# The last of seven down products moved behind the classical rest, and the memory sums in half-size transfers over more of the layer

## The chip, the cores and the metric

The kernel runs on one core of one Trainium2 chip. The metric is device time in microseconds of one execution; lower is better. Besides the times there is one profiled execution with its trace, on which the figures below rest.

## The reference

A two-layer encoder over 512 rows of width 1024, in float32. Each layer, cut to what matters here:

```
h   = rms_norm(x, pre_mix_norm)
q, k, v, u, B, C = split(h @ w_in)            # 6 x 512 columns
attn = dilated_mixture_attention(rotary(q), rotary(k), v)
conv = B * short_conv(C * u)
x   = x + rms_norm(concat(rms_norm(attn), rms_norm(conv)) @ w_out, post_mix_norm)
g, u = split(rms_norm(x, pre_ffn_norm) @ w_gate_up)      # 2 x 2816 columns
x   = x + rms_norm((silu(g) * u) @ w_down, post_ffn_norm)
```

## The kernel before

**Numbers and tiles.** Rows are held in four tiles of 128 (t = 0 to 3), the width in eight k tiles, the hidden width of 2816 in 22 tiles m. Every factor is split in two fp32r parts, hi and lo, so a product of two tiles is three matmuls (hi by hi, hi by lo, lo by hi). Weights arrive as halves of 128 x 1024 float32, 512 KB: `load_raw` issues the load on the SP queue (line 122), `split_half` makes hi on ScalarE (line 221) and lo on VectorE (line 222). Three raw buffers and four buffers each of hi and lo rotate. `take_half` splits up to two halves ahead of the one it returns, and `split_half` loads up to two halves ahead of that; the argument `keep` names the oldest half that must stay because a later row tile reads it again.

**Who orders what.** TensorE and SP run in the order in which the code issues their work. The order on ScalarE, VectorE and POOL is set by a planner that simulates costs, with program order as priority; instructions under `keep_in_program_order` stay in order among themselves.

**The layer's stages.** The input projection begins with the values (function `values`, called for a row tile and a half of the k tiles), goes on with four pairs of query/key tiles and six pairs of convolution tiles, and runs attention in steps in between: each k step calls `advance`. Then come the output projection, the gate/up product and the down product. The gate/up product takes tiles m = 0 to 3 classically and m = 4 to 21 by seven products of half size in place of eight (function `seven`, matmuls at line 900); for each such m two halves are loaded and seven weight operands are made.

**The down product.** The first 16 of the 22 hidden tiles also go by seven products of half size (function `partial`, matmuls at line 994), the other six (the rest, `REST = 6`) classically (line 1056), into the same PSUM banks. A block (two row tiles by 512 columns) of the output is called c11, c12 (rows 0 and 1, first and second half of the columns), c21, c22 (rows 2 and 3). Product p = 0 to 6 holds 48 matmuls over eight k tiles for two row tiles. The activation operands of product p are made by `operands(p)` while product p-1 runs; product six adds to c21 only. `rest_splits` splits the activations of the six rest tiles. After product six the rest runs for f = 0, 1 (column halves) and t = 0 to 3, 18 matmuls each; after each the block is evacuated (square with row sum, multiplication with the gain); after f = 1 the row tile is finished: scale, residual (line 689), and where a layer follows, its norm (`normed`, lines 292 and 294).

**The turn to the next layer.** `transposed` turns one row tile of the normalised rows with eight transposes on TensorE (line 301), and splits the result (lines 305, 306). Row tiles 0 and 1 are turned in the rest pass f = 1, after three hidden tiles of t = 2 and of t = 3. Row tiles 2 and 3 are turned in the next layer's values, in the calls (0, 1) and (1, 1) after two k tiles.

**The memory sums.** Four of the seven weight operands of the down product are sums of weight blocks. They are made in device memory: t1 = b11 + b12, t3 = b12 + b22, t2 = t1 + b22, t4 = t2 + b21, by transfers from memory to memory that POOL issues, some plain, some adding (`weight_sums`). A block is 2 MB and goes in two transfers of 1 MB, 16 transfers a layer. So that they don't start at once, each is tied to a place in SP's order: SP issues a load of four bytes (`due`, line 158, into a slot of the pool `small`, which the softmax and the norms use too), POOL copies it (line 159) and then issues the transfer (line 160). `feed_forward` calls `next(adding)` after each of the 18 seven-product tiles.

Of the kernel before, what the change touches and what calls it, by code (L numbers as in the profile page):

```python
# [36 lines left out]
KS = 8  # L37
SB = 7 * KS // 2
REST = MT - 2 * KS
EPS = 1e-6  # L40
MAGIC = 12582912.0

# [40 lines left out]
def encoder(ctx: ExitStack, tc: tile.TileContext, x, xT, pos, mask, cols, rows, w, wd, out):  # L83
# [48 lines left out]
    def weight_source(i):  # L132

        l, r = divmod(i, 2 * NCHUNK)
        if r < 2 * NW:
            return w[l * NW + r // 2][:, (r % 2) * 1024:(r % 2) * 1024 + 1024]
        p, q = divmod(r - 2 * NW, KS // 2)
        if p < 7:
            src = (lambda: down_quarter(l, 0, 0), lambda: tsum[l][:, 0, :], lambda: tsum[l][:, 1, :],
                   lambda: down_quarter(l, 1, 0), lambda: tsum[l][:, 2, :], lambda: down_quarter(l, 1, 1),  # L140
                   lambda: tsum[l][:, 3, :])[p]()
            return src[:, q * 1024:q * 1024 + 1024]
        c = 4 * KS * 512 + (r - 2 * NW - SB) * 1024
        return wd[l][:, c:c + 1024]

    def weight_sums(l):

        b11, b12, b21, b22 = (down_quarter(l, g, f) for g in range(2) for f in range(2))  # L150
        t1, t2, t3, t4 = (tsum[l][:, k, :] for k in range(4))
        for pairs in (((t1, b11), (t3, b12)), ((t1, b12), (t3, b22)), ((t2, t1),), ((t2, b22),), ((t4, t2),), ((t4, b21),)):
            for n, (o, src) in enumerate(pairs):
                for c in range(0, KS * 512, 2048):
                    add = {"accum_op": ALU.add} if src is b22 or src is b21 or (src is b12 and o is t1) else {}
                    due = small(1)[:1]
                    seen = sb.tile([1, 1], F32, tag="seen", bufs=2, name=nm("seen"))
                    nc.sync.dma_start(due, cols[0:1, 0, 0:1])
                    tc.keep_in_program_order(nc.gpsimd.tensor_copy(seen, due))
                    tc.keep_in_program_order(nc.gpsimd.dma_start(o[:, c:c + 2048], src[:, c:c + 2048], **add))  # L160
                    yield

    tc.keep_in_program_order(nc.scalar.preload_act_table_set("trig_and_small"))
# [120 lines left out]
    def new_hT():  # L284
        return [[big([P, 4, S], F32R) for _ in range(2)] for _ in range(2)]
# [11 lines left out]
    def transposed(t, h, hT, tag, raw=None):  # L297
        for g in range(2):
            b = bank(tag)
            for k in range(4):  # L300
                nc.tensor.transpose(b[:, k * P:(k + 1) * P], h[:, (4 * g + k) * P:(4 * g + k + 1) * P], ident)
            b4 = b.rearrange("p (k t) -> p k t", k=4)
            hi = hT[0][g][:, :, t * P:(t + 1) * P]
            lo = hT[1][g][:, :, t * P:(t + 1) * P]
            nc.scalar.copy(hi, b4)
            nc.vector.tensor_sub(lo, b4, hi.bitcast(F32))
            if raw is not None:
                nc.scalar.copy(raw[g][:, :, t * P:(t + 1) * P], b4)
# [288 lines left out]
                nc.scalar.activation(V[:, t, :], accs[t], AF.Copy, scale=inv[:, 2 * t:2 * t + 1])  # L597
        return inv

    def in_proj_attention(l, hT, h, tables):  # L600

        base = l * NCHUNK
        V = big([P, NT, S])
# [2 lines left out]
        def values(t, g, turn=None):  # L606
            if accs[t] is None:
                accs[t] = bank("acc")
            for kt in range(4 * g, 4 * g + 4):
                if turn is not None and kt == 4 + TURN // 2:  # L610
                    transposed(turn, h[turn], hT, "acc")
                hi, lo = take(base + g, (kt % 4) // 2, 2 * base if t < NT - 1 else None)
                c = (kt % 2) * 512
                mm3(accs[t], hT[0][g][:, kt % 4, t * P:(t + 1) * P], hT[1][g][:, kt % 4, t * P:(t + 1) * P],
                    hi[:, c:c + 512], lo[:, c:c + 512], kt == 0, kt == KT - 1)
            if g == 1:
                nc.scalar.copy(V[:, t, :], accs[t])

        inv = None
        if l == 0:  # L620
            inv = first_values(hT, V)
            nc.sync.dma_start(mask_sb, mask)
        else:
            for o in [(0, 0), (0, 1, 2), (1, 0), (1, 1, 3), (2, 0), (2, 1), (3, 0), (3, 1)]:
                values(*o)

        qks = [None] * 4
# [4 lines left out]
        count = [0]  # L632

        def advance():
            for _ in range(PACE[count[0] % len(PACE)]):
                next(att, None)
            run_background(BG)
            count[0] += 1
# [104 lines left out]
    def feed_forward(l, hT, hs, raw, adding):  # L743
# [35 lines left out]
        def gated_full(m, accs):  # L779
            sg = tmp([P, S])  # L780
            nc.scalar.activation(sg, accs[0], AF.Silu)
            gated(m, sg, accs[1])
# [159 lines left out]
        for m in range(3):  # L942
            pair_part(base + m, accs[m], hT, HS, S, step, keep if m == 0 else None)
            gated_full(m, accs[m])
        ahead = None
        for m in range(3, SEVEN):
            n = [0]
# [38 lines left out]
        def partial(p, outs, start, ahead):  # L986
            hi_t, lo_t = seconds.pop(p)
            for k in range(KS):
                wh, wl = take_half(d0 + p * (KS // 2) + k // 2)
                c = (k % 2) * 512  # L990
                for i in range(2):
                    st = slice(i * P, i * P + P)
                    for n, (sh, mh) in enumerate(((hi_t, wh), (hi_t, wl), (lo_t, wh))):
                        nc.tensor.matmul(outs[i], sh[:, k, st], mh[:, c:c + 512], start=start and k == 0 and n == 0,  # L994
                                         stop=False, skip_group_check=True)
                next(ahead, None)
            for _ in ahead:
                pass

        def rest_splits():  # L1000
            for m in range(2 * KS, MT):
                split(m)
                yield
# [23 lines left out]
        c22.extend((written("att", 5), written("pv", 5)))  # L1027
        for i in range(2):
            nc.vector.tensor_sub(c22[i], p5[i], c21[i])
        partial(5, c12, False, operands(6))  # L1030
        for i in range(2):
            nc.vector.tensor_sub(c12[i], c12[i], u2[i])
        partial(6, c21, False, rest_splits())
        accs = [c11 + c21, c12 + c22]

        def evac(f, t, acc):
            j = row([P, S])
            nc.scalar.activation(j, acc, AF.Square, accum_out=ssq[t][:, f:f + 1])
            fx[f][t] = (row if f else tmp)([P, S])
            nc.vector.tensor_mul(fx[f][t], acc, gpost[:, f * 512:f * 512 + 512])  # L1040

        log_table()
        for f in range(2):
            if f == 1 and gnext is not None:
                hT = new_hT()
            for t in range(NT):
                for m in range(2 * KS, MT):
                    j = f * REST + m - 2 * KS
                    if m == 2 * KS + TURN_D and f == 1 and gnext is not None and t >= 2:
                        transposed(t - 2, hs[t - 2], hT, "acc")  # L1050
                        hs[t - 2] = None
                    wh, wl = take_half(d0 + SB + j // 2, d0 + SB + f * REST // 2 if t < NT - 1 else None)
                    c = (j % 2) * 512
                    hi, lo = act_dst(m)
                    for n, (sh, mh) in enumerate(((hi, wh), (hi, wl), (lo, wh))):
                        nc.tensor.matmul(accs[f][t], sh[:, t * P:(t + 1) * P], mh[:, c:c + 512], start=False,  # L1056
                                         stop=m == MT - 1 and n == 2, skip_group_check=True)
                evac(f, t, accs[f][t])
                if f == 0:
                    part0[t] = mean_part(ssq[t][:, 0:1], D)  # L1060
                else:
                    r = rsqrt_mean(ssq[t][:, 1:2], D, part=part0[t])
                    residual(t, fx, r)
                    if gnext is not None:
                        hs[t] = normed(t, gnext)
                    else:
                        nc.sync.dma_start(out[t * P:(t + 1) * P, :512], x_sb[t][:, :512])
                        nc.scalar.dma_start(out[t * P:(t + 1) * P, 512:], x_sb[t][:, 512:])
        return hT, hs

    with tc.manual_schedule(engines={mybir.EngineType.PE, mybir.EngineType.SP}):
        warm_up()
        hs = [None] * NT
        hT = new_hT()
        tables = None
        for l in range(DEPTH):
            adding = weight_sums(l)
            merged, sq_a, sq_c, tables, inv = in_proj_attention(l, hT, hs, tables)
            hT, hs, raw = out_proj(l, merged, sq_a, sq_c, inv)
            hT, hs = feed_forward(l, hT, hs, raw, adding)  # L1080

# [87 lines left out]
```

## Time and profile before

| what | value |
|---|---|
| time, median of three runs | 1168.9 us (1167.38 to 1169.53) |
| the profiled execution: time / span | 1170.38 us / 1168.4 us |
| granted TensorE clock, mean | 0.997 |
| busy: TensorE / VectorE / ScalarE / POOL | 98% / 72% / 57% / 6% of the span |
| moved by DMA | 162.64 MB, mean 139 GB/s |
| memory sums in it: plain or adding from the weights / from a sum | 24 / 8 transfers of 1 MB, two layers |

The span is from the first to the last instruction. In a row of the TensorE timeline stand the start, the duration, the line, the operation with output and inputs, and in brackets the idle time before it with what ended it; matmuls are pipelined, so a row's duration is longer than the distance to the next start. A row of a window shows its length, then the busy time and count of TensorE, its weight loads, VectorE, ScalarE and POOL, then the granted clock, the share of the DMA engines and GB/s. A row of waits has the total, the number and the longest. A row of the chain of waits has the start, the length and what the chain ran through.

### The profile page before, as it was taken

Reading aid. Unit: us, or ns where it says so; the run is one execution under the profiler, and the core shown is the slowest. Engines: PE = TensorE matmul, PEld = TensorE weight load, DVE = VectorE, ACT = ScalarE, POOL = GpSimd, SP = SyncE. Lnnn points to the kernel's source line nnn. Section 1 sums busy time; section 2 is a strip of 40 time slices with the busy share of each in tenths; the row PEclk is TensorE's granted clock in tenths of the full one; section 3 lists DMA queues with packets and bytes.
Section 4 is the critical chain, followed back from the end, with each engine's and each line's share of the span. In section 5 each row is a group of like instructions: output and inputs, shape, how many; then the busy total and the mean of one; then the engine's idle time right before and its main releaser. Section 6 shows DMA issues by size and latency. Waiting matters only on the chain.

```text
span 1168.4 us, 18250 instructions
## 1 busy us (share of the span) xinstructions
PE 1148.5 (98%) x7008; PEld 1010.5 (86%) x7008; DVE 841.4 (72%) x1392; ACT 669.8 (57%) x1263; POOL 70.0 (6%) x127
## 2 busy tenths in 40 slices
PE   9999999999999999999999999999999999999997
PEld 8777778899999999888777777788999999998886
DVE  5798664776886778984757986448767777789844
ACT  7577544564655656663545775446545556567632
POOL 6000011000010000000000000110000011000000
PEclk9999999999999999999999999999999999999999
DMA  8221234222677777665223212441136776676641
GB/s 323 91 72 55 73 90 126 74 73 90 206 185 191 213 216 181 217 203 176 69 66 100 73 55 72 126 125 53 59 125 193 203 196 182 207 181 213 198 144 73
DMA packets 41911, 162.64 MB, mean 139 GB/s; under 512 B 4960, under 2 KB 4960, under 8 KB 37728
## 3 DMA queue, kind: packets, MB, share of 16 engines
q1 hardware_dynamic: 35344, 122.64, 32.8%
q0 software_dynamic: 5760, 37.75, 13.7%
q8 instruction: 55, 0.90, 0.3%
q10 hardware_dynamic: 720, 1.09, 0.3%
q14 instruction: 32, 0.26, 0.1%
HBM read 159.36 MB, written 35.65 MB: 167 GB/s over the span
## 4 chain that ended last, share of the span: by engine, by line
PE 44%; DVE 3%; DMA 2%; ACT 1%; issue 1%; DVEq 0%; ACTq 0%; SPq 0%
PE acc L900 7%; PE att L900 6%; PE acc L250 5%; PE acc L251 5%; PE acc L252 5%; PE acc L994 5%; PE att L994 2%; DMA raw<-in_w 2%; PE acc L1056 1%; PE pv L487 1%; PE att L480 1%; PE att L1056 1%; PE att L250 1%; PE att L252 1%; PE att L251 1%
## 5 line engine op out<-in xcount | busy, mean ns | idle before, releaser
L222 DVE TENSOR_TENSOR wl<-raw,wh 128x1024 fp32r<-128x1024 f32 x140 | 170.7, 1220 | 79.3 <-ACT wh L221 78.2
L900 PE MATMUL acc<-big,wh 128*128 128x256 f32 x1152 | 212.2, 283 | 0.0
L221 ACT CAST wh<-raw 128x1024 fp32r<-128x1024 f32 x140 | 146.9, 1051 | 108.8 <-PE acc L251 35.9
L900 PEld LDWEIGHTS acc<-big,wh 128*128 128x128 f32 x1152 | 179.8, 192 | 0.2
L900 PE MATMUL acc<-big,wl 128*128 128x256 f32 x576 | 163.7, 284 | 2.8 <-DVE wl L821 2.8
L900 PE MATMUL att<-big,wh 128*128 128x256 f32 x864 | 160.7, 283 | 0.2 <-ACT att L908 0.2
L250 PE MATMUL acc<-big,wh 128*128 128x512 f32 (+1 forms) x400 | 154.0, 385 | 0.0
L252 PE MATMUL acc<-big,wl 128*128 128x512 f32 (+1 forms) x400 | 149.5, 374 | 0.0
L251 PE MATMUL acc<-big,wh 128*128 128x512 f32 (+1 forms) x400 | 149.3, 373 | 0.0
L900 PEld LDWEIGHTS att<-big,wh 128*128 128x128 f32 x864 | 134.6, 192 | 0.5 <-ACT att L908 0.4
L900 PE MATMUL att<-big,wl 128*128 128x256 f32 x432 | 123.2, 285 | 0.4
L820 ACT CAST wh<-t 128x512 fp32r<-128x512 f32 x144 | 88.7, 619 | 45.8 <-PE att L900 30.7
L900 PEld LDWEIGHTS acc<-big,wl 128*128 128x128 f32 x576 | 110.5, 192 | 3.9 <-DVE wl L821 3.7
L821 DVE TENSOR_TENSOR wl<-t,wh 128x1024 fp32r<-128x1024 f32 x72 | 87.7, 1218 | 17.3 <-ACT wh L820 17.3
L994 PE MATMUL acc<-wh,big 128*128 128x512 f32 x320 | 99.5, 389 | 0.0
L820 ACT CAST wh<-raw 128x512 fp32r<-128x512 f32 x108 | 63.4, 619 | 47.0 <-PE acc L900 31.3
L252 PEld LDWEIGHTS acc<-big,wl 128*128 128x128 f32 x400 | 75.3, 188 | 13.9
L250 PEld LDWEIGHTS acc<-big,wh 128*128 128x128 f32 x400 | 75.4, 189 | 12.3 <-issue 0.8
L251 PEld LDWEIGHTS acc<-big,wh 128*128 128x128 f32 x400 | 75.6, 189 | 11.6
L900 PEld LDWEIGHTS att<-big,wl 128*128 128x128 f32 x432 | 82.8, 192 | 2.2 <-DVE wl L821 2.2
L821 DVE TENSOR_TENSOR wl<-raw,wh 128x512 fp32r<-128x512 f32 x72 | 68.5, 951 | 6.2 <-ACT wh L820 6.0
L994 PEld LDWEIGHTS acc<-wh,big 128*128 128x128 f32 x320 | 60.1, 188 | 12.4
(265 smaller groups left out, 2225.5 us busy)
## 6 DMA issues: line engine op xcount, KB each, us to landing
raw<-in_w SPq DMA_DIRECT2D x144, 512.0 KB
tsum<-in_wd POOLq DMA_DIRECT2D x24, 1024.0 KB, 8.1
raw<-in_wd SPq DMA_DIRECT2D x36, 512.0 KB
raw<-tsum SPq DMA_DIRECT2D x32, 512.0 KB
tsum<-tsum POOLq DMA_DIRECT2D x8, 1024.0 KB, 5.3
gain<-in_rows SPq DMA_DIRECT2D x7, 512.0 KB
big<-in_xT SPq DMA_DIRECT2D x8, 256.0 KB
raw<-in_w SPq DMA_DIRECT2D x8, 256.0 KB
```

Source lines behind the costliest of these rows:

```text
L221: nc.scalar.copy(hi, raws[i])
L222: nc.vector.tensor_sub(lo, raws[i], hi.bitcast(F32))
L250: nc.tensor.matmul(o, sh, mh, start=start, stop=False)
L251: nc.tensor.matmul(o, sh, ml, start=False, stop=False)
L252: nc.tensor.matmul(o, sl, mh, start=False, stop=stop)
L480: nc.tensor.transpose(tp[:, k * P:(k + 1) * P], sm[:, k * P:(k + 1) * P], ident)
L487: nc.tensor.matmul(o[hd * 64:hd * 64 + 64, half * 256:half * 256 + 256], V[:, k, hc:hc + 64], PT[hd][:, k, :], start=k == 0, stop=k == NT - 1)
L820: nc.scalar.copy(hi[:, c:c + 512], src[:, c:c + 512])
L821: nc.vector.tensor_sub(lo[:, :n], src[:, :n], hi[:, :n].bitcast(F32))
L900: nc.tensor.matmul(o[:, :HS], sh[:, c], mh[:, k, :], start=start and k == 0 and n == 0, stop=k == 3 and n == 2, skip_group_check=True)
L994: nc.tensor.matmul(outs[i], sh[:, k, st], mh[:, c:c + 512], start=start and k == 0 and n == 0, stop=False, skip_group_check=True)
L1056: nc.tensor.matmul(accs[f][t], sh[:, t * P:(t + 1) * P], mh[:, c:c + 512], start=False, stop=m == MT - 1 and n == 2, skip_group_check=True)
```

## The change

The change has two parts.

First, the down product: the rest now runs right after product five, f = 0 and then f = 1, and product six comes last, its two row tiles (t = 2 and t = 3, columns of f = 0) one after the other, 24 matmuls each with the four weight halves held for both. Row tiles 0 and 1 are finished in the rest pass f = 1 as before; row tiles 2 and 3 are evacuated for f = 1 there and finished after their part of product six. Row tiles 0 and 1 are turned in the middle of product six's first and second part, row tiles 2 and 3 in the values of the next layer at (1, 0) and (2, 0), after two k tiles; the banks for the turned rows come from the tag `att` and no more from `acc`. The order in which the weight halves are loaded follows (`SR`), and `before_rest` makes the operands of product six and the rest splits during product five.

Second, the memory sums: 32 transfers of 512 KB a layer in place of 16 of 1 MB, in the same order, and 11 of them are tied to steps of the input projection (every sixth `advance`), 3 to the tiles m = 0 to 2 of gate/up, 18 to the seven-product tiles.

```diff
     def weight_source(i):
...
-        p, q = divmod(r - 2 * NW, KS // 2)
+        r -= 2 * NW
+        if SR <= r < SR + REST:
+            c = 4 * KS * 512 + (r - SR) * 1024
+            return wd[l][:, c:c + 1024]
+        p, q = divmod(r if r < SR else r - REST, KS // 2)
...
     def weight_sums(l):
-                for c in range(0, KS * 512, 2048):
+                for c in range(0, KS * 512, 1024):
...
-                    tc.keep_in_program_order(nc.gpsimd.dma_start(o[:, c:c + 2048], src[:, c:c + 2048], **add))
+                    tc.keep_in_program_order(nc.gpsimd.dma_start(o[:, c:c + 1024], src[:, c:c + 1024], **add))
                     yield
...
         def values(t, g, turn=None):
-                if turn is not None and kt == 4 + TURN // 2:
-                    transposed(turn, h[turn], hT, "acc")
+                if turn is not None and kt == TURN // 2:
+                    transposed(turn, h[turn], hT, "att")
...
-            for o in [(0, 0), (0, 1, 2), (1, 0), (1, 1, 3), (2, 0), (2, 1), (3, 0), (3, 1)]:
+            for o in [(0, 0), (0, 1), (1, 0, 2), (1, 1), (2, 0, 3), (2, 1), (3, 0), (3, 1)]:
                 values(*o)
...
         def advance():
+            if count[0] % 6 == 5:
+                next(adding, None)
...
         for m in range(3):
             pair_part(base + m, accs[m], hT, HS, S, step, keep if m == 0 else None)
             gated_full(m, accs[m])
+            next(adding, None)
...
-        partial(5, c12, False, operands(6))
+        def before_rest():
+            for _ in operands(6):
+                yield
+            for _ in rest_splits():
+                yield
+
+        partial(5, c12, False, before_rest())
         for i in range(2):
             nc.vector.tensor_sub(c12[i], c12[i], u2[i])
-        partial(6, c21, False, rest_splits())
         accs = [c11 + c21, c12 + c22]
...
+        def finished(t, f):
+            r = rsqrt_mean(ssq[t][:, f:f + 1], D, part=part0[t])
+            residual(t, fx, r)
+            if gnext is not None:
+                hs[t] = normed(t, gnext)
+            else:
+                nc.sync.dma_start(out[t * P:(t + 1) * P, :512], x_sb[t][:, :512])
+                nc.scalar.dma_start(out[t * P:(t + 1) * P, 512:], x_sb[t][:, 512:])
+
+        def turned(t):
+            if gnext is not None:
+                transposed(t, hs[t], hT, "att")
+                hs[t] = None
...
         for f in range(2):
             for t in range(NT):
                 for m in range(2 * KS, MT):
-                    if m == 2 * KS + TURN_D and f == 1 and gnext is not None and t >= 2:
-                        transposed(t - 2, hs[t - 2], hT, "acc")
-                        hs[t - 2] = None
-                    wh, wl = take_half(d0 + SB + j // 2, d0 + SB + f * REST // 2 if t < NT - 1 else None)
+                    wh, wl = take_half(d0 + SR + j // 2, d0 + SR + f * REST // 2 if t < NT - 1 else None)
...
-                evac(f, t, accs[f][t])
-                if f == 0:
+                if f == 0 and t < 2:
+                    evac(0, t, accs[0][t], tmp)
                     part0[t] = mean_part(ssq[t][:, 0:1], D)
+                elif f == 1:
+                    evac(1, t, accs[1][t], row if t < 2 else tmp)
+                    if t < 2:
+                        finished(t, 1)
+                    else:
+                        part0[t] = mean_part(ssq[t][:, 1:2], D)
+
+        if gnext is not None:
+            hT = new_hT()
+        hi_t, lo_t = seconds.pop(6)
+        for i in range(2):
+            for k in range(KS):
+                if k == KS // 2:
+                    turned(i)
+                wh, wl = take_half(d0 + SR + REST + k // 2, None if i else d0 + SR + REST)
+                c = (k % 2) * 512
+                st = slice(i * P, i * P + P)
+                for n, (sh, mh) in enumerate(((hi_t, wh), (hi_t, wl), (lo_t, wh))):
+                    nc.tensor.matmul(c21[i], sh[:, k, st], mh[:, c:c + 512], start=False,
+                                     stop=k == KS - 1 and n == 2, skip_group_check=True)
+            evac(0, 2 + i, c21[i], row)
+            finished(2 + i, 0)
         return hT, hs
```

More of the change, by code (lines that the diff above doesn't have):

```diff
@@ L39 @@
 REST = MT - 2 * KS
+SR = 6 * KS // 2
 EPS = 1e-6
@@ L142, in weight_source @@
             return src[:, q * 1024:q * 1024 + 1024]
-        c = 4 * KS * 512 + (r - 2 * NW - SB) * 1024
-        return wd[l][:, c:c + 1024]
     def weight_sums(l):
@@ L598, in first_values, with in_proj_attention @@
         return inv
-    def in_proj_attention(l, hT, h, tables):
+    def in_proj_attention(l, hT, h, tables, adding):
         base = l * NCHUNK
@@ L1029, in feed_forward, with evac @@
             nc.vector.tensor_sub(c22[i], p5[i], c21[i])
-        partial(5, c12, False, operands(6))
+        def before_rest():
[4 more added lines that the diff above has]
+        partial(5, c12, False, before_rest())
         for i in range(2):
             nc.vector.tensor_sub(c12[i], c12[i], u2[i])
-        partial(6, c21, False, rest_splits())
         accs = [c11 + c21, c12 + c22]
-        def evac(f, t, acc):
+        def evac(f, t, acc, tag):
             j = row([P, S])
             nc.scalar.activation(j, acc, AF.Square, accum_out=ssq[t][:, f:f + 1])
-            fx[f][t] = (row if f else tmp)([P, S])
+            fx[f][t] = tag([P, S])
             nc.vector.tensor_mul(fx[f][t], acc, gpost[:, f * 512:f * 512 + 512])
+        def finished(t, f):
[10 more added lines that the diff above has]
+                hs[t] = None
         log_table()
         for f in range(2):
-            if f == 1 and gnext is not None:
-                hT = new_hT()
             for t in range(NT):
@@ L1056, in feed_forward @@
                         nc.tensor.matmul(accs[f][t], sh[:, t * P:(t + 1) * P], mh[:, c:c + 512], start=False,
-                                         stop=m == MT - 1 and n == 2, skip_group_check=True)
-                evac(f, t, accs[f][t])
-                if f == 0:
+                                         stop=(f == 1 or t < 2) and m == MT - 1 and n == 2, skip_group_check=True)
+                if f == 0 and t < 2:
+                    evac(0, t, accs[0][t], tmp)
                     part0[t] = mean_part(ssq[t][:, 0:1], D)
[L1061 to L1065, printed above, removed]
-                    else:
-                        nc.sync.dma_start(out[t * P:(t + 1) * P, :512], x_sb[t][:, :512])
-                        nc.scalar.dma_start(out[t * P:(t + 1) * P, 512:], x_sb[t][:, 512:])
+                elif f == 1:
+                    evac(1, t, accs[1][t], row if t < 2 else tmp)
+                    if t < 2:
+                        finished(t, 1)
+                    else:
+                        part0[t] = mean_part(ssq[t][:, 1:2], D)
[14 more added lines that the diff above has]
+            finished(2 + i, 0)
         return hT, hs
@@ L1077, in encoder @@
             adding = weight_sums(l)
-            merged, sq_a, sq_c, tables, inv = in_proj_attention(l, hT, hs, tables)
+            merged, sq_a, sq_c, tables, inv = in_proj_attention(l, hT, hs, tables, adding)
             hT, hs, raw = out_proj(l, merged, sq_a, sq_c, inv)
```

## The prediction

> **What bounds the kernel now.** I read the head of the page first, then the list of what TensorE waited for over the whole run.
>
> ```profile
> span 1168.4 us, 18250 instructions
> ...
> PE 1148.5 (98%) x7008; PEld 1010.5 (86%) x7008; DVE 841.4 (72%) x1392; ACT 669.8 (57%) x1263; POOL 70.0 (6%) x127
> ```
>
> ```profile
> PE acc L301 <- DVE small L273: 3.6, 2, 2.1
> PE acc L900 <- DVE wl L821: 2.8, 4, 1.0
> PE acc L301 <- DVE small L269: 1.5, 3, 1.2
> ```
>
> TensorE sets the time, and no change that leaves its matmuls alone can win more than its holes. The three longest entries stand in two places: L301, the transposes that carry the normalised rows into the next layer, and L900, the seven-product part of gate/up. A busy figure hides slow matmuls, so I measured both places by their start times, with the TensorE timeline, the chain of waits and the windows by stage.
>
> **Place one, the border between the layers**, from the first rest matmul of layer 0 (L1056) to the first matmul after the values of layer 1:
>
> ```profile
> 545.78 0.39 PE L1056 MATMUL acc<-wh,big 128*128 128x512 f32 x1
> ...
> 573.98 1.06 PE L301 MATMUL acc<-ident,mid 128*128 128x128 f32 x8 [1.51 <-DVE small L273]
> ...
> 580.36 1.07 PE L301 MATMUL acc<-ident,mid 128*128 128x128 f32 x8 [1.21 <-DVE small L269]
> ...
> 589.78 1.49 PE L301 MATMUL acc<-ident,mid 128*128 128x128 f32 x8 [2.13 <-DVE small L273]
> ...
> 597.80 1.03 PE L301 MATMUL acc<-ident,mid 128*128 128x128 f32 x8
> 598.60 0.47 PE L250 MATMUL acc<-wh,big 128*128 128x512 f32 x1
> ...
> 610.96 0.39 PE L250 MATMUL acc<-big,wh 128*128 128x512 f32 x1
> ```
>
> ```profile
> 590.00:594.00 4.00, 4.00 (x16) 3.36 (x15) 3.04 (x7) 2.44 (x7) 0.00 (x0) 0.57 0.27 103
> ```
>
> ```profile
> 1128.87 16.32 PE acc L1056 x72
> ...
> 1161.55 0.69 ACT row L1038 x2
> ```
>
> The undisturbed pace is 16.32 / 72 = 0.2267 us a matmul. The stretch holds 144 rest and 96 value matmuls, 54.4 us, and four turns of eight transposes, which cost 0.88 us each where nothing waits (598.60 - 597.80, and 0.08 for the slower matmul behind): 57.9 us. It took 610.96 - 545.78 = 65.2 us. The loss is **7.25 us**: 4.85 us of waiting before three turns, and most of the rest is the clock, granted at 0.57 from 590 to 594 us, right behind the 2.13 us hole.
>
> **Place two, the 18 seven-product tiles of each layer**, first and last matmul of both layers, the pace in a clean part, one window of it, and the queues:
>
> ```profile
> 284.98 0.40 PE L900 MATMUL acc<-big,wh 128*128 128x256 f32 x2
> ```
>
> ```profile
> 468.69 0.40 PE L994 MATMUL acc<-wh,big 128*128 128x512 f32 x1
> ```
>
> ```profile
> 864.85 0.40 PE L900 MATMUL acc<-big,wh 128*128 128x256 f32 x2
> ```
>
> ```profile
> 1051.61 0.40 PE L994 MATMUL acc<-wh,big 128*128 128x512 f32 x1
> ```
>
> ```profile
> 875.09 2.88 PE acc L900 x24
> ...
> 885.17 2.88 PE acc L900 x24
> ...
> 1025.62 7.25 DMA raw<-in_w
> ```
>
> ```profile
> 870.00:960.00 90.00, 90.00 (x752) 90.00 (x751) 67.65 (x94) 53.21 (x116) 8.40 (x18) 1.00 0.69 194
> ```
>
> ```profile
> 357.99 3.31 SPq L122 DMA_DIRECT2D raw<-in_w  x2
> 361.35 0.28 SPq L158 DMA_DIRECT2D small<-in_cols  x1
> 369.38 3.31 SPq L122 DMA_DIRECT2D raw<-in_w  x2
> ```
>
> ```profile
> tsum<-in_wd POOLq DMA_DIRECT2D x24, 1024.0 KB, 8.1
> ```
>
> A clean tile takes 885.17 - 875.09 = 10.08 us, so 18 take 181.4 us. Layer 0 took 183.7 and layer 1 186.8: losses of **2.27 and 5.32 us**. Their cause is the supply of weights. The SP queue issued its weight pairs 11.39 us apart (357.99 to 369.38) where a tile lasts 10.08. Such a pair waits for a buffer, lands beside a 1 MB memory sum (8.1 us to land) and is split; prefetch covers this for a while, and then the chain shows a load of 7.25 us on the path. The two places hold 14.84 us together.
>
> **The change part by part.** *Matmuls.* None is added or removed: 48 matmuls of product six run after the rest passes as two groups of 24, one per row tile. The pace of a product is that of the rest, 10.88 us for 48 in the row below and 0.2267 us each, so 0.
>
> *The rest begins one product earlier.* Its operands must be split during product five instead of six, on top of the operands of product six. These rows say whether that time is there, the last rest split on VectorE and product five's start in layer 1:
>
> ```profile
> 1095.54 1.28 DVE L757 TENSOR_TENSOR big<-mid,big 128x512 fp32r<-128x512 f32 x2
> ```
>
> ```profile
> 1107.11 10.88 PE att L994 x48
> ```
>
> The planner already put the last rest split at 1096.8, 10 us before product five even begins and 21 us before the rest would begin now (1107.11 + 10.88). Cost 0; without that lead it would be at most the six splits, 6 x 0.64 = 3.9 us a layer.
>
> *Where the rows are turned.* What counts is the distance, in TensorE work, from a tile's last matmul to its transposes. Before, t=0 had 18 + 9 matmuls (6.1 us), t=1 the same and a turn (7.0), t=2 36 and a turn (9.0), t=3 42 and a turn (10.4). After, t=0 is finished in the second rest pass and turned in the middle of product six's first half: 54 + 12 matmuls, 15.0 us; t=1 has 36 + 24 + 12 and a turn, 17.2 us; t=2 and t=3, finished by product six, have 54 and a turn each, 13.1 us. The work between, from the square on ScalarE to the normalised rows on VectorE, is shown by the first and the last tile:
>
> ```profile
> 566.44 0.60 ACT L1038 ACTIVATE row<-att 128x512 f32<-128x512 f32 x1 [2.43 <-PE att L1056]
> ```
>
> ```profile
> 572.55 1.28 DVE L294 SCALAR_TENSOR_TENSOR mid<-x,small,gain 128x1024 f32<-128x1024 f32 x1
> ```
>
> ```profile
> 583.54 0.60 ACT L1038 ACTIVATE row<-pv 128x512 f32<-128x512 f32 x1 [0.32 <-PE pv L1056]
> ```
>
> ```profile
> 595.35 1.28 DVE L294 SCALAR_TENSOR_TENSOR mid<-x,small,gain 128x1024 f32<-128x1024 f32 x1
> ```
>
> It took 7.4 us for t=0 (566.44 to 573.83) and 13.1 us for t=3 (583.54 to 596.63), with VectorE crowded. Before, every distance lay under its need or near it; after, t=0 and t=1 have twice the need and t=2, t=3 just the crowded one. All four holes should close, and the slow clock with them.
>
> What is late next is VectorE. Before, the last rest tile ran on weights split long before; now four halves of product six and four of the values follow each other at 1.36 us of TensorE each (product six holds each half for 6 matmuls at a time), so about seven splits of 1.2 us fall into the 20 us in which three rows are normalised. It was tight already: in the before run a split ended at 586.18 and the matmul that reads it started at 586.29.
>
> ```profile
> 584.95 1.23 DVE L222 TENSOR_TENSOR wl<-raw,wh 128x1024 fp32r<-128x1024 f32 x1
> ```
>
> ```profile
> 586.29 0.44 PE L251 MATMUL acc<-wl,big 128*128 128x512 f32 x1
> ```
>
> I bound what stays of place one between 0 (all hidden) and 5 us (each of seven splits one 0.69 us VectorE operation late) and take **1.5**, nearer to nothing, since the distances of the rows leave the planner room to put splits first.
>
> *The memory sums.* Before, 16 transfers of 1 MB a layer fell into 18 tiles; after, 11 of 32 halves go out in the input projection, 3 before the tiles and 18 in them: 9 MB of 16. In the clean window 194 GB/s moved; the weights are 1 MB a tile, 104 GB/s, the sums the other 90. At 9/16 they move 51, together 155. A load that lands in 7.25 us beside them scales to 5.8 us; the worst loop of 11.39 us becomes about 9.9, under the 10.08 of TensorE. That is the good end. Against it, other POOL transfers of 512 KB landed hardly faster than 1 MB:
>
> ```profile
> wk<-in_w POOLq DMA_DIRECT2D x4, 512.0 KB, 6.1
> big<-in_w POOLq DMA_DIRECT2D x4, 512.0 KB, 5.0
> ```
>
> But landing time holds latency in which nothing moves, and what delays a weight is the moving. I keep **2.0 us** of the 7.59, between 0 (every loop under 10.08) and 7.6 (nothing changes), nearer to the bytes because the stage is full of them.
>
> The Trainium skill speaks against this edit: "DMA: Bandwidth & Descriptors", sections "Anatomy of one DMA" and "Rules for kernel authors", gives a POOL transfer a fixed 2 us beside its bytes and asks for 1 MiB or more. By its formula 512 KB is 3.2 us and 1 MB 4.4, so the sums in a tile would fall only from 16/18 x 4.4 = 3.9 to 3.2 us and most of place two would stay. The two rows above lean its way.
>
> *What the input projection gets.* Eleven sums a layer move to a stage whose engines look like this in layer 1, and so do eleven small loads on SP, each followed by a copy and an issue on POOL:
>
> ```profile
> 620.00:740.00 120.00, 119.34 (x629) 93.96 (x628) 95.56 (x213) 81.68 (x154) 5.53 (x5) 1.00 0.21 66
> ```
>
> DMA is at 0.21 and POOL at 5.5 of 120 us, so the transfers are covered; uncovered, one would delay a weight half by at most its own 8.1 us. Queued behind a POOL wait are the additions of squares, first needed by the row scales after the stage. I take 0.5 us for both layers, between 0 and 2. In layer 1 the SP queue also stands at the output stores of t=0 and t=1 before it issues product six's last half; that half is first read 36 + 18 matmuls, 12.2 us, after t=1's last one, and the whole longer chain to normalised rows took 7.4, so 0.
>
> *The tail.* From the last matmul (square at 1161.55) to the end are 6.85 us of the same operations as before: 0.
>
> **Sum:** 14.84 - 1.5 - 2.0 - 0.5 = 10.8 us less. The profiled execution was 1170.38 us, 2.0 beyond its span; it would become 1159.6. The median of the runs shown, 1168.9, is 1.5 us below that execution and becomes **1158.1**.
>
> **The rivals.**
>
> *VectorE takes over at the border.* The end of place one's estimate: 5 us stay, gain 10.8 - 3.5 = 7.3, **1161.6 us**. For it: the split that was 0.1 us early. Against: t=0 and t=1 no longer compete there.
>
> *Half the size, not half the time.* If a 512 KB sum holds the DMA engines as long as a 1 MB one, place two stays whole: 10.8 - 5.6 = 5.2, **1163.7 us**. For it: each tile still carries one sum, and the 5.0 and 6.1 us above. Against: the stage moved bytes at 194 GB/s, so bytes count there. This is the course that the Trainium skill's "DMA: Bandwidth & Descriptors" points to.
>
> *SP held in the input projection, slower.* Each sum's small load takes a slot of the pool that the softmax uses, and SP issues in order: a load that stands for such a slot holds the weights behind it. The SP queue's waits and the end of the stage:
>
> ```profile
> SPq L122 <- DVE small L473: 72.6, 8, 11.7
> ```
>
> ```profile
> 774.41 0.79 PE att L544 x8
> ```
>
> SP already stands up to 11.7 us at a softmax operation. From 610.96 to 774.41 are one pair of halves without attention (10.9 us), nine with it and 24 matmuls (5.4 us): 16.3 us a pair, 8.2 a half. A hold longer than that is paid by TensorE, 11.7 - 8.2 = 3.5 us each time. Four hits of 22 more than eat the gain; seven, 24.5 us, make **1182.6 us**. For it: the pool is shared. Against: 24 slots reach eight scores back, and TensorE lost under 1 us of 120 in the window above.
>
> **How the numbers follow.** Forecast 0.70, VectorE 0.12, size 0.11, SP held 0.05, and 0.02 that small gains and small holds cancel. The low end is every hole closed: 1168.9 - 14.8 = 1154.1. Both milder rivals together would leave 10.8 - 3.5 - 5.6 = 1.7, 1167.2 us; I stop the range at 1166, a little inside. 1154 to 1166 then holds the forecast and each milder rival alone. 0.2%, 2.3 us, is about what a measurement of this kernel can tell from no change: faster 0.91, within it 0.03, slower 0.06.
>
> **What would show it.** In the changed profile the waits at L301's transposes should be gone or under 0.5 us each, and no border window should show a clock under 1.00. From the first rest matmul to the first after the values there are then 288 matmuls and four turns, 65.3 + 3.5 = 68.8 us; up to 71 is as forecast. Each seven-product stage should last under 183 us, with SP's pairs about 10.1 us apart, and the input projection should keep its length to 1 us. Wrong would be waits on weight splits at product six or the values (the first rival), stages of 184 and 187 us with loads on the chain (the second), or an input projection longer by several us behind SP (the third).

## The result, and the profile after

The changed kernel takes **1157.8 us** (median of 4 runs, 1157.5 to 1157.9) against 1168.7 us before (4 runs on the same chip): a ratio of 0.9907, 95% interval 0.989 to 0.9924. The forecast was 1158.1 us, between 1154 and 1166.

What TensorE waited for, in the changed kernel; L305 is now the line of the transposes and L906 that of the seven-product tiles:

```profile
PE acc L255 <- DVE wl L226: 1.3, 1, 1.3
...
PE acc L305 <- DVE small L273: 0.4, 2, 0.2
```

The three longest entries of before are gone: L906 is not in the list at all, and the 0.4 us before transposes lie in the output projections, none at this border. One new entry has come, 1.3 us for a weight split.

The border between the layers, from the first rest matmul to the first matmul after the values, on the TensorE timeline (start, duration, line, operation):

```profile
532.33 0.39 PE L1001 MATMUL att<-wh,big 128*128 128x512 f32 x1
532.56 0.39 PE L1079 MATMUL acc<-wh,big 128*128 128x512 f32 x1
...
567.93 1.03 PE L305 MATMUL att<-ident,mid 128*128 128x128 f32 x8
...
574.26 1.03 PE L305 MATMUL att<-ident,mid 128*128 128x128 f32 x8
...
583.69 0.50 PE L255 MATMUL acc<-wl,big 128*128 128x512 f32 x1 [1.34 <-DVE wl L226]
...
586.32 1.04 PE L305 MATMUL att<-ident,mid 128*128 128x128 f32 x8
...
592.68 1.03 PE L305 MATMUL att<-ident,mid 128*128 128x128 f32 x8
...
603.09 0.39 PE L254 MATMUL acc<-big,wh 128*128 128x512 f32 x1
```

All four turns follow without a wait. The stretch now includes product six and lasts 70.53 us, 1.7 over the 68.8 that its 288 matmuls and four turns need; before, the loss was 7.25. One hole is left, before L255, in the values. The clock stays at 1.00 through the border, also in the window with the hole (the last three columns are granted clock, DMA share and GB/s):

```profile
580.00:592.00 12.00, 10.66 (x52) 8.57 (x51) 8.51 (x19) 5.36 (x13) 0.00 (x0) 1.00 0.42 134
```

The seven-product tiles, first and last matmul of layer 1, and what SP and the DMA engines did in them (layer 0's stage runs from 284.81 to 466.35, the same 181.54 us):

```profile
857.07 0.40 PE L906 MATMUL acc<-big,wh 128*128 128x256 f32 x2
```

```profile
1038.61 0.40 PE L1001 MATMUL acc<-wh,big 128*128 128x512 f32 x1
```

```profile
346.35 3.42 SPq L124 DMA_DIRECT2D raw<-in_w  x2
349.82 0.28 SPq L162 DMA_DIRECT2D small<-in_cols  x1
356.43 3.43 SPq L124 DMA_DIRECT2D raw<-in_w  x2
```

```profile
857.00:1038.00 181.00, 181.00 (x1509) 180.90 (x1508) 145.50 (x196) 109.17 (x234) 16.86 (x34) 1.00 0.58 155
```

Each stage takes 181.54 us where 18 clean tiles are 181.4. The weight pairs go out 10.08 us apart, the pace of TensorE itself, and the stage moves 155 GB/s at a DMA share of 0.58.

### The profile page after: what moved, and what is told of

Read it like the earlier page. It is cut to its first block, busy times and chain, and to the rows that moved or that the text cites. A ratio compares the mean times of both kernels' runs of the same rounds, so it can differ in the third digit from the quotient of the medians.

```text
span 1155.4 us, 18407 instructions
## 1 busy us (share of the span) xinstructions
PE 1142.4 (99%) x7008; PEld 1008.2 (87%) x7008; DVE 846.5 (73%) x1392; ACT 670.9 (58%) x1263; POOL 111.0 (10%) x191
## 4 chain that ended last, share of the span: by engine, by line
PE 95%; DVE 2%; ACT 2%; issue 1%; DVEq 0%; ACTq 0%
PE acc L906 18%; PE att L906 13%; PE acc L255 9%; PE acc L254 9%; PE acc L256 9%; PE acc L1001 8%; PE att L1001 4%; PE acc L1079 3%; PE pv L491 3%; PE att L484 2%; PE att L1079 2%; PE att L254 2%; PE att L256 2%; PE att L255 2%; PE att L467 1%; PE acc L1103 1%
## 5 line engine op out<-in xcount | busy, mean ns | idle before, releaser
L906 PE MATMUL acc<-big,wh 128*128 128x256 f32 x1152 | 212.0, 283 | 0.0
L906 PEld LDWEIGHTS acc<-big,wh 128*128 128x128 f32 x1152 | 179.8, 192 | 0.2
L906 PE MATMUL acc<-big,wl 128*128 128x256 f32 x576 | 163.0, 283 | 0.0
L906 PE MATMUL att<-big,wh 128*128 128x256 f32 x864 | 160.3, 283 | 0.0
L255 PE MATMUL acc<-big,wh 128*128 128x512 f32 (+1 forms) x400 | 149.4, 373 | 0.0
L906 PEld LDWEIGHTS att<-big,wh 128*128 128x128 f32 x864 | 134.7, 192 | 0.1
L906 PE MATMUL att<-big,wl 128*128 128x256 f32 x432 | 122.2, 283 | 0.0
L906 PEld LDWEIGHTS acc<-big,wl 128*128 128x128 f32 x576 | 110.6, 192 | 0.0
L163 POOL COPY seen<-small 1x1 f32<-1x1 f32 x64 | 30.8, 481 | 753.1 <-DMA small<-in_cols 753.1
L255 PEld LDWEIGHTS acc<-big,wh 128*128 128x128 f32 x400 | 75.6, 189 | 11.6
L906 PEld LDWEIGHTS att<-big,wl 128*128 128x128 f32 x432 | 82.9, 192 | 0.0
L1001 PE MATMUL acc<-wh,big 128*128 128x512 f32 x256 | 79.4, 389 | 0.0
```

The lines of the kernel that those rows point to most:

```text
L255: nc.tensor.matmul(o, sh, ml, start=False, stop=False)
L906: nc.tensor.matmul(o[:, :HS], sh[:, c], mh[:, k, :], start=start and k == 0 and n == 0, stop=k == 3 and n == 2, skip_group_check=True)
```

## The experiments

Times are medians of 4 to 11 runs, each beside the kernel before on the same chip (1168.8 to 1169.1 us). Lengths of stages come from the profiled execution of each kernel, read as above. "Down and border" is from the end of layer 0's seven-product tiles to the first matmul after layer 1's values, so that both orders of the down product cover the same 142.3 us before and 136.7 us in the changed kernel; without any hole it would be 57.9 + 77.1 = 135.0.

| kernel | time, us | down and border | tiles, layer 0 | tiles, layer 1 |
|---|---|---|---|---|
| before | 1168.7 | 142.3 | 183.7 | 186.8 |
| changed | 1157.8 | 136.7 | 181.5 | 181.5 |
| down_only | 1164.6 | 136.8 | 183.9 | 186.4 |
| sums_only | 1162.9 | 142.2 | 181.6 | 181.5 |
| half_in_tiles | 1167.6 | 136.7 | 185.1 | 188.6 |
| full_spread | 1157.1 | 136.8 | 181.6 | 181.5 |
| later_turns | 1156.4 | 135.5 | 181.6 | 181.6 |
| turn_short | 1160.1 | 140.0 | 181.5 | 181.5 |
| values_order | 1155.8 | 135.1 | 181.6 | 181.6 |
| all_in_proj | 1162.6 | 136.7 | 181.6 | 181.6 |
| all_in_proj_1mb | 1162.7 | 136.7 | 181.5 | 181.6 |
| values_spread | 1156.2 | 137.1 | 181.6 | 181.5 |
| later_spread | 1156.7 | 135.6 | 181.6 | 181.6 |

### Each part alone: down_only and sums_only

down_only takes the sums back:

```diff
-                for c in range(0, KS * 512, 1024):
+                for c in range(0, KS * 512, 2048):
...
-            if count[0] % 6 == 5:
-                next(adding, None)
...
             gated_full(m, accs[m])
-            next(adding, None)
```

> Only the down product is changed; the sums stay 16 transfers of 1 MB a layer in the seven-product tiles. If the border and the tile stages are two separate losses, the border closes as in the changed kernel (70.5 us instead of 65.2 + 10.9 = 76.1, a gain of 5.5 us) and the tile stages keep about 183.7 and 186.8 us: about 1163.2 us. If the sums also slowed the border or the changed border helps the stages, the stages move by more than 1 us or the gain is not 5.5.

Measured: 1164.6 us (ratio 0.9957, 0.9944 to 0.9969). The border is that of the changed kernel and the tile stages are those of before, 183.9 and 186.4 us.

sums_only is the kernel before with the new `weight_sums` and its three places, and the old down product.

> Only the sums are changed; the down product stays in the old order. Separate losses: the tile stages fall to 181.5 us each (a gain of 7.5 us in the profile), the border keeps its 65.2 us with three holes: about 1162 us. If the two parts need each other, it stays above 1164.

Measured: 1162.9 us (0.9937, 0.9923 to 0.995). The three old holes stand, within 0.02 us of their old lengths and of their old distances from the first rest matmul:

```profile
PE acc L301 <- DVE small L273: 3.6, 2, 2.1
PE acc L301 <- DVE small L269: 1.5, 3, 1.2
```

So the two losses are separate. Alone they give 4.3 and 6.0 us, together 10.3 of the 11.0.

### Bytes or size of the sums: half_in_tiles and full_spread

half_in_tiles keeps the halves but issues all in the seven-product tiles, with no `next(adding)` elsewhere; full_spread keeps the spread but in 1 MB transfers, at every twelfth `advance`, behind tiles 0 and 2 and behind every second seven-product tile. At these tiles, first half_in_tiles, then full_spread:

```diff
             seven(m, ys[m % 2], ahead)
-            next(adding, None)
+            for _ in range(2):
+                next(adding, None)
...
             seven(m, ys[m % 2], ahead)
-            next(adding, None)
+            if m % 2:
+                next(adding, None)
```

> The changed kernel with 32 transfers of 512 KB a layer, but all of them in the seven-product tiles, two a tile. If the bytes in the stage delay the weights (my reason), the stages lose again what they lost before, 2 to 5 us each, and the time is about 1163 us. If the size of one transfer delays them, the stages stay at 181.5 us and the time at 1157.8.

> The changed kernel with 16 transfers of 1 MB a layer, 5 in the input projection, 2 before the tiles and 9 in every second tile: the same bytes in the stage as in the changed kernel, the old size. If the bytes decide, 1157.8 us and stages of 181.5. If the size decides, the tiles with a transfer lose as before and the time is 1160 to 1163.

Measured: 1167.6 us (0.9982, 0.9973 to 0.9992) and 1157.1 us (0.9895, 0.9881 to 0.9908). The stage of layer 1 in down_only (1 MB, all in the tiles), in half_in_tiles and in full_spread:

```profile
860.00:1045.00 185.00, 182.61 (x1503) 180.62 (x1502) 141.80 (x195) 107.94 (x233) 15.14 (x32) 1.00 0.68 191
```

```profile
861.00:1048.00 187.00, 183.26 (x1501) 180.65 (x1500) 141.28 (x194) 107.76 (x233) 27.87 (x64) 1.00 0.69 189
```

```profile
857.00:1038.00 181.00, 181.00 (x1510) 180.94 (x1509) 145.42 (x198) 108.75 (x234) 7.93 (x16) 1.00 0.51 152
```

The bytes decide: at 190 GB/s TensorE waits, at 155 or less it does not, with transfers of either size. Nothing between 155 and 189 GB/s was run. Nor is it the number of transfers: in layer 1 down_only starts 16 of them in the stage and TensorE waits, the changed kernel starts 17 and it does not. My estimate for half_in_tiles was too good by 4.6 us, since it left out that halves cost more: with the same 16 MB in the tiles the stages of half_in_tiles lose 3.4 us more than 1 MB transfers (185.1 + 188.6 against 183.9 + 186.4), and the share of the DMA engines is 0.58 against 0.51 where the spread is the same. The times to landing fit this, though that they are the cause is not shown; half_in_tiles also has twice the small loads on SP, and its sums start in pairs:

```profile
tsum<-in_wd POOLq DMA_DIRECT2D x48, 512.0 KB, 5.6
```

Half the size lands in 5.6 us, packed as in half_in_tiles or spread as in the changed kernel; 1 MB took 8.1 us in down_only and 8.6 in full_spread. In direction this is what the Trainium skill says ("DMA: Bandwidth & Descriptors", "Rules for kernel authors", 1 MiB or more). The halving in this change wins nothing: full_spread, with 1 MB, is as fast.

### Is it the distance of the turns: later_turns and turn_short

later_turns has the old order of the down product, product six before the rest, with the new sums; only the turns come later:

```diff
-                    if m == 2 * KS + TURN_D and f == 1 and gnext is not None and t >= 2:
-                        transposed(t - 2, hs[t - 2], hT, "acc")
-                        hs[t - 2] = None
+                    if m == 2 * KS + TURN_D and f == 1 and gnext is not None and t == 3:
+                        transposed(0, hs[0], hT, "acc")
+                        hs[0] = None
...
-            for o in [(0, 0), (0, 1, 2), (1, 0), (1, 1, 3), (2, 0), (2, 1), (3, 0), (3, 1)]:
+            for o in [(0, 0), (0, 1, 1), (1, 0), (1, 1, 2), (2, 0), (2, 1, 3), (3, 0), (3, 1)]:
```

> The old order of the down product (product six before the rest) with the new sums, and only the turns moved later: t=0 after three hidden tiles of t=3 in the rest, t=1, t=2 and t=3 in the values at (0, 1), (1, 1) and (2, 1), so 45 matmuls (10.2 us) behind t=0's last one and 54, 60 and 66 and a turn (13.1 to 15.9 us) for the others. Compare with 1162.9 us for the new sums alone. If the distance is what closed the border, the three holes and the slow clock go here too: about 1157.5 us. If product six at the end is needed, the border keeps its loss: 1161 to 1163.

Measured: 1156.4 us (0.9891, 0.9878 to 0.9905), down and border 135.5 us. All holes of the border are gone, and the weight split is in time too, although product six runs where it always ran. The four turns follow without a wait:

```profile
575.04 1.03 PE L301 MATMUL acc<-ident,mid 128*128 128x128 f32 x8
...
582.23 1.03 PE L301 MATMUL acc<-ident,mid 128*128 128x128 f32 x8
...
588.83 1.03 PE L301 MATMUL acc<-ident,mid 128*128 128x128 f32 x8
...
595.18 1.03 PE L301 MATMUL acc<-ident,mid 128*128 128x128 f32 x8
```

The time holds about 1 us from the start of layer 0, which the edit does not touch: one wait there is 0.8 us in place of 0.2, and the tiles begin at 285.79 instead of 284.8 us. Why the order came out differently there is not known.

turn_short is the changed kernel with t=2 and t=3 turned earlier:

```diff
-            for o in [(0, 0), (0, 1), (1, 0, 2), (1, 1), (2, 0, 3), (2, 1), (3, 0), (3, 1)]:
+            for o in [(0, 0, 2), (0, 1), (1, 0, 3), (1, 1), (2, 0), (2, 1), (3, 0), (3, 1)]:
```

> The changed kernel with the turn of t=2 at (0, 0) and of t=3 at (1, 0) in the values, so t=2's distance falls from 13.1 to 7.7 us (30 matmuls and a turn). In the changed kernel t=2 took 10.6 us from its square to its normalised rows. If distance against that chain sets the holes, one hole of about 3 us opens before t=2's turn, with some 1.5 us of slow clock behind it, while the 1.34 us hole is hidden by it: about 1160.5 us. If the planner just follows the need, no hole: 1157.8.

Measured: 1160.1 us (0.9921, 0.9908 to 0.9935). The chain of t=2 again took 10.6 us, from its square at 571.71 to its normalised rows at 582.35, though they were needed earlier. The hole is there, in the size that the distance gives (10.6 - 7.7 = 2.9), and the slow clock behind it:

```profile
582.49 1.94 PE L305 MATMUL att<-ident,mid 128*128 128x128 f32 x8 [3.11 <-DVE small L277]
```

```profile
582.00:586.00 4.00, 3.51 (x13) 3.16 (x14) 3.45 (x7) 1.56 (x3) 0.00 (x0) 0.57 0.70 213
```

Both together settle the border: what counts is how much TensorE work lies between a row tile's last matmul and its turn. Moving product six to the end is one way to get it; moving the turns alone is another and gives at least as much.

### The hole that was left: values_order

The last hole waits for the split of the fourth values half. VectorE in the changed kernel around it, then ScalarE:

```profile
577.89 2.36 DVE L226 TENSOR_TENSOR wl<-raw,wh 128x1024 fp32r<-128x1024 f32 x2
...
580.97 0.20 DVE L273 TENSOR_SCALAR small<-small,small 128x1 f32<-128x1 f32 x1
581.09 1.28 DVE L298 SCALAR_TENSOR_TENSOR mid<-x,small,gain 128x1024 f32<-128x1024 f32 x1
582.29 0.21 DVE L277 SCALAR_TENSOR_TENSOR small<-small,small 128x1 f32<-128x1 f32 x1
582.42 1.22 DVE L226 TENSOR_TENSOR wl<-raw,wh 128x1024 fp32r<-128x1024 f32 x1
```

```profile
571.73 0.60 ACT L1051 ACTIVATE row<-acc 128x512 f32<-128x512 f32 x1 [1.52 <-PE acc L1103]
...
580.07 1.05 ACT L225 CAST wh<-raw 128x1024 fp32r<-128x1024 f32 x1 [0.40 <-DMA raw<-in_w]
```

The split starts behind the norm of t=2 (L298, 1.28 us); 0.4 us more come from its load, which ScalarE waited for. The same rows show the chain of t=2, from its square at 571.73 to the end of L298 at 582.37; 2.4 of its 10.6 us are two other weight splits that VectorE did in between (577.89). values_order uses the half later:

```diff
-                if turn is not None and kt == TURN // 2:
+                if turn is not None and kt == 4 * g + TURN // 2:
...
-            for o in [(0, 0), (0, 1), (1, 0, 2), (1, 1), (2, 0, 3), (2, 1), (3, 0), (3, 1)]:
+            for o in [(0, 0), (1, 0), (0, 1, 2), (1, 1), (2, 0, 3), (2, 1), (3, 0), (3, 1)]:
```

> The changed kernel; the values run (0, 0), (1, 0), (0, 1), (1, 1), so the third and fourth weight halves are needed 12 matmuls, 2.7 us, later; the turns keep their distance. If the hole of 1.34 us that is left at the border is a split one VectorE operation late, it goes: about 1156.3 us. If the planner moves the split back with the need, it stays: 1157.8.

Measured: **1155.8 us** (0.9884, 0.9871 to 0.9898), the border 68.90 us, from

```profile
532.48 0.39 PE L1079 MATMUL acc<-wh,big 128*128 128x512 f32 x1
```

```profile
601.38 0.39 PE L254 MATMUL acc<-big,wh 128*128 128x512 f32 x1
```

which is 0.1 over the need. It is the fastest kernel of the study.

### How much the input projection can take: all_in_proj and all_in_proj_1mb

```diff
-            if count[0] % 6 == 5:
+            if count[0] % 2 == 1:
```

> The changed kernel with all 32 sums of a layer tied to the input projection, one every second step, three times as many small loads on SP and waits on POOL there. If they cost what I took (0.5 us for 22), it stays within 2 us of 1157.8. If SP is held by the softmax's slots, or the sums' 16 MB delay the weights of that stage, the input projection grows by several us: 1165 or more.

Measured: 1162.6 us (0.994, 0.9926 to 0.9953), 4.8 more than the changed kernel. Attention itself is not slowed: the first matmul of the output projection starts at 188.87 us, in the changed kernel at 188.75. The holes come behind it, in the output projection, and up to the tiles 2.7 us are lost in layer 0 and 2.2 in layer 1. ScalarE, VectorE, TensorE, POOL and one window there, in layer 0:

```profile
191.12 1.06 ACT L238 ACTIVATE big<-big 128x1024 fp32r<-128x1024 f32 x1 [10.96 <-DMA big<-in_w]
```

```profile
193.15 1.23 DVE L226 TENSOR_TENSOR wl<-raw,wh 128x1024 fp32r<-128x1024 f32 x1 [12.21 <-ACT wh L225]
```

```profile
198.85 0.50 PE L254 MATMUL acc<-wh,big 128*128 128x512 f32 x1 [0.71 <-DVE tmp L540]
...
217.54 0.50 PE L255 MATMUL att<-wl,big 128*128 128x512 f32 x1 [0.76 <-DVE wl L226]
```

```profile
183.95 0.84 POOL L164 DMA_DIRECT2D tsum<-in_wd  x1 [0.25 <-issue]
192.47 0.91 POOL L239 DMA_DIRECT2D big<-in_w  x1 [7.67 <-ACT big L238]
```

```profile
150.00:200.00 50.00, 49.19 (x240) 38.76 (x239) 22.85 (x35) 17.69 (x27) 17.42 (x28) 1.00 0.90 225
```

The DMA engines are at 0.90 in this window (0.45 in the kernel before, 0.63 in the changed one), and a weight transfer of POOL for gate/up (`split_by_dma`) lands late among the last sums: POOL issued it 2.2 us later than in the changed kernel (177.59 against 175.36), and ScalarE could use it 6.5 us later (191.12 against 184.66). ScalarE stands 11 us at it with a split of the output projection queued behind, VectorE stands 12 us at that split, and the last convolution queued behind it on VectorE comes late: TensorE waits for its last operation (L540), and further on for a weight split. It is not SP at the softmax's slots, as my slower rival had it: SP's small loads stood there 51.3 us in 17 waits, 5.2 us at most, and attention lost nothing.

all_in_proj_1mb does the same with 16 transfers of 1 MB, one every fourth step.

> The changed kernel with all sums in the input projection as 16 transfers of 1 MB, one every fourth step. With 32 halves there the first weight transfer that POOL issues for gate/up came late (ScalarE stood 11 us at it) and the time was 1162.6 us. If the cause is that the sums take longer than the stage, and halves cost more than their bytes, it is better here, 1158 to 1160 us. If the bytes alone fill the stage, it stays at 1162.

Measured: 1162.7 us (0.9942, 0.9929 to 0.9954), DMA share in the same window 0.90. The larger transfers do not help here: of the two courses expected, it is the one of the bytes, with 228 GB/s in the window.

### Both helpful edits at once: values_spread and later_spread

values_spread is values_order with the 1 MB spread, later_spread is later_turns with it.

> The changed kernel with both edits that helped: the values' order (1155.8 us) and 16 transfers of 1 MB spread over the layer (1157.1). The order removes the last border hole, and the transfers change nothing that TensorE waits for, so their 0.6 us should not add fully: 1155.2 to 1155.8 us.

> The old order of the down product, the turns moved later (1156.4 us) and 16 transfers of 1 MB spread over the layer. If the move of product six adds nothing once the turns are late, it ends with the kernel that has the values' order and this spread, within 1 us: 1155 to 1156.5 us.

Measured: 1156.2 us (0.9883, 0.9868 to 0.9898; runs from 1155.5 to 1157.7) and 1156.7 us (0.9891, 0.9877 to 0.9904; 1156.1 to 1157.9). Neither beats values_order by what can be told. With the sums spread, their size is worth nothing that these runs can tell, and the two orders of the down product end within 1 us of each other. The profiled execution of values_spread, the slowest of its four at 1157.7 us, is not free of waits for weights: behind its last sum ScalarE stands 8.45 us at a load of a sum, and two holes of 0.55 and 0.46 us open before weight splits early in the down product, which makes the 137.1 us in the table.

## Why the prediction was right

**The places.** Two losses with separate causes: right, and each part alone closes its own. down_only and sums_only came within 1.4 and 0.9 us of what was expected of them.

**The border, 1.5 of 7.25 us left.** 1.7 stayed. The mechanism was the one named: distance against the chain of square, scale, residual and norm. The rows t=2 and t=3 needed 10.6 us (square at 571.73, norm done at 582.37) and 9.7 us, not the crowded 13.1 that I compared with 13.1; so the distance had 2.5 us to spare for t=2. What was late next was, as written, a weight split one VectorE operation late, only it was one split and not several: 1.34 us.

**The rest one product earlier, 0.** Right: the first rest matmul (532.56) follows the last of product five (532.33) at the usual pace.

**The tile stages, 2.0 of 7.59 us left.** This term was mis-sized. By the bytes, 155 GB/s and a loop under 10.08 us, I had computed that nothing would stay, and exactly that came: 155 GB/s, 10.08 us, 0.2 us left in both stages. The 2.0 was put in for 512 KB transfers that land hardly faster than 1 MB; landing time is indeed long, as half_in_tiles shows, but at 155 GB/s TensorE does not wait for it.

**The input projection, 0.5.** It was 0: in layer 1, from the first matmul after the values to the tiles, 253.98 us against 253.89. The cover that I named, a DMA share of 0.21, was enough for 11 sums a layer; all_in_proj shows that it is not for 32, and what that costs.

**The tail, 0.** Right: from the start of the last matmul to the end 7.28 us against 7.27, and the down product of layer 1 ahead of it, from the end of the tiles, 109.50 against 109.51.

**The sum.** In the profile the change won 12.9 us (1170.38 to 1157.52), 2.1 more than the sum of 10.8, mostly the 1.8 of the tile stages. The median moved by 11.0. The difference lies in the kernel before: its runs range from 1167.4 to 1172.6 us over all comparisons, where those of the changed kernel lie between 1157.5 and 1157.9, and the profiled one stood 1.7 above the median. That the waits for weights are what varies is likely: down_only and half_in_tiles, which keep all sums in the tiles, spread over 3.8 and 3.0 us, the changed kernel over 0.4. It was not measured run by run. So the median was hit within 0.4 us partly by luck, because two errors had opposite signs: too much loss left in the tiles, and a loss taken from a run that had more of it than most.

**The rivals.** VectorE at the border appeared with about a third of its price. Half the size is indeed not half the time to landing, but that has no effect that can be told once the sums are spread. The slower rival did not appear, not even with all 32 sums in the input projection; what gave way there was ScalarE at a POOL transfer, and the loss was under 5 us.

## What to carry to other kernels

Where a row chain separates two stages, count the matmuls between a tile's last product and the first use of its result, and compare them with the chain's length in the trace; if the distance is short, try moving the use, which cost nothing here, before moving work. Where weights stream, compare a stage's GB/s with stages that wait and stages that do not (here 190 and 155): move bytes to a stage that has room, don't cut transfers without a reason, and look for what is queued behind the last of them.

## What the runs showed of the hardware that was not expected

The granted clock fell after holes of 2.1 us and longer: 0.57 in the four microseconds behind the 2.13 us hole of before, 0.57 behind the 3.11 us hole of turn_short (its window stands above), and in sums_only behind one of 2.11 us:

```profile
588.00:592.00 4.00, 4.00 (x15) 3.29 (x14) 2.62 (x7) 2.86 (x8) 0.00 (x0) 0.59 0.19 70
```

Behind holes of 1.2 to 1.5 us, in before and in the changed kernel, it stayed at 1.00. In before, the matmuls behind the hole started 0.43 us apart instead of 0.227 until 593.63, 1.6 us in all, so that the hole of 2.1 us cost 3.7. The Trainium skill ("TensorE: Matmul & The Clock Gate", "Why this matters for your kernels") puts the limit for idle time at about 3 us. The wait of 2.13 us lies below it; from the end of the last matmul (587.66) to the first one behind the transposes (590.92) it is 3.3 us. Which of the two lengths counts, and whether the holes of 1.5 and 1.2 us in the 16 us before had a part, no run here separates.

The drop does not seem to come every time. Of the five runs of sums_only three have a mean clock of 0.997 and take 1162.9 to 1163.1 us; two have 0.999 and take 1161.2 and 1161.4, 1.6 us less, which is the price of the slow matmuls. Only one of the three was profiled, so that the clock stayed up behind the hole in the other two is likely but not shown.
